# Seven-product steps of a decoder trunk: four weight sums by VectorE subtractions, against three VectorE additions and one accumulating DMA

## The chip, the core and the metric

The kernel runs on one core of a Trainium2 chip. The metric is the device time of one execution in microseconds (us), the median over runs. Before the change it is 2035.99 us (3 runs, 2035.79 to 2036.19).

Names of the engines in the profile: PE is TensorE (PEld its weight loads), DVE is VectorE, ACT is ScalarE, POOL is GpSimd, SP is the engine that issues most DMAs here.

## What is computed

A decoder trunk of two layers over a sequence of 256 tokens with a model width of 2048, all in float32:

```
for l in range(DEPTH):                                   # 2
    h = rms_norm(x, norm1_g[l])
    z = h @ w_in[l]                                      # 2048 x 5120
    ... attention heads and gated groups -> mix
    x = x + mix @ w_out[l]                               # 2048 x 2048
    h2 = rms_norm(x, norm2_g[l])
    x = x + jnp.square(jax.nn.relu(h2 @ w_up[l])) @ w_down[l]   # 2048 x 8192, 8192 x 2048
return rms_norm(x, final_g)
```

The change is inside the product with `w_down`.

## The kernel before

**Splitting.** Each float32 weight and activation is split into a high part (`hi`, rounded to the fast matmul type by an ACT copy, line 160) and a low part (`lo`, the value less its high part, a DVE subtraction, line 170). A product is three matmuls: hi x hi, hi x lo, lo x hi. The weights come in blocks of 128 x 1024 numbers (512 KB), one DMA per block from the SP queue (line 151) into a `raw` buffer, of which there are six. There are seven `hi` buffers and six `lo` buffers. A block's `raw` buffer is free again when its `lo` is made.

**Steps.** The program is a list of steps. An ordinary step has one block: 24 matmuls of 128 x 256. A *seven-product step* (function `fast`) has two loaded blocks, which hold a 2 x 2 grid of weight sub-blocks, and makes 7 instead of 8 sub-products of it by the Strassen-Winograd scheme: 7 products of 6 matmuls each. For that it needs four sums of weights. They are made in place in the two loaded blocks, and the two blocks are then split a second time as if they were new blocks. So a seven-product step has four entries in the list of blocks: before the change `Top`, `Bottom`, and two `Sums`, here called *upper* and *lower*. Each entry takes one `hi` and one `lo` buffer. The activations' sums (function `sums`) and the final combination of the seven products (function `combine`) are made by DVE too. The seventh product of a step is left over and done inside the next step.

**Where they stand.** In each layer the MLP runs over nine rounds `e` (0 to 8); round `e` has 16 ordinary steps for `w_up` and works on the hidden columns of round `e - 1` for `w_down`: in rounds 1 to 7 four seven-product steps and 8 ordinary steps, in round 8 two and 12. That is 30 seven-product steps in a layer, 60 in all. In rounds 2 to 7 they are put ahead of the `w_up` steps numbered 1, 2, 6 and 13, so the first two of them have a single ordinary step between them. In round 1 they stand at 7, 10, 14 and 15.

**What sets the order.** Each engine runs its instructions in the order in which the program issues them. Ahead of a step's matmuls the program calls `high_to`, which issues ACT copies for blocks up to six entries ahead, and then `low_to`, which issues DVE subtractions up to five entries ahead (fewer at the program's start). The entries of a `Sums` first issue the DVE sums, and ahead of these `high_to` makes sure that the low parts which still need the unsummed block are issued. Other work (updates of `x`, the `relu` square of the hidden columns at lines 733, 734, 629, 630, the sum of kept products at line 805) is put between the steps by small queues.

Of the kernel before, what the change touches and what calls it, by code (L numbers as in the profile page):

```python
# [85 lines left out]
def trunk(ctx: ExitStack, tc: tile.TileContext, layout, xT, consts, gains, w, b_sp, w_sp, out):  # L86
    nc = tc.nc
# [9 lines left out]
    vec, act, pe = nc.vector, nc.scalar, nc.tensor  # L97
# [9 lines left out]
    inner = ar[:, 0:2048].rearrange("p (k t) -> p k t", k=NH)  # L107
# [29 lines left out]
    class Sub:  # L137


        loads, frees = True, 1  # L140

        def __init__(self, *spec):
            self.i = len(layout)
            self.kc, self.n = spec[-2:]
            layout.append(spec)
# [7 lines left out]
        def high(self, parts, between=None):  # L153
            self.h = wp.tile([P, 1024], F32R, name="hi", tag="hi", bufs=HI_BUFS)
            self.hi = self.h.rearrange("p (k n) -> p k n", n=self.n)
            m = 1024 // parts
            for j in range(parts):
                if between and j:
                    between()
                act.activation(self.h[:, j * m:(j + 1) * m], self.raw[:, j * m:(j + 1) * m], AF.Copy)  # L160

        def low(self, parts, between=None):
            lo = wp.tile([P, 1024], F32R, name="lo", tag="lo", bufs=LO_BUFS)
            self.lo = lo.rearrange("p (k n) -> p k n", n=self.n)
            m = 1024 // parts
            for j in range(parts):
                r = slice(j * m, (j + 1) * m)
                if between and j:
                    between()
                vec.tensor_tensor(lo[:, r], self.raw[:, r], self.h[:, r].bitcast(F32), op=OP.subtract)  # L170

    class Top(Sub):


        def high(self, parts):
            h = wp.tile([P, 1024], F32R, name="hi", tag="hi", bufs=HI_BUFS)
            self.hi = h[:, 0:512].rearrange("p (k n) -> p k n", k=2)
            act.activation(self.hi, self.left(), AF.Copy)

        def low(self, parts):  # L180
            lo = wp.tile([P, 1024], F32R, name="lo", tag="lo", bufs=LO_BUFS)
            self.lo = lo[:, 0:512].rearrange("p (k n) -> p k n", k=2)
            vec.tensor_tensor(self.lo, self.left(), self.hi.bitcast(F32), op=OP.subtract)

        def left(self):
            return self.raw.rearrange("p (k n) -> p k n", k=2)[:, :, 0:256]

        def right(self):
            return self.raw.rearrange("p (k n) -> p k n", k=2)[:, :, 256:512]

        frees = 0

    class Bottom(Sub):


        left, right, frees = Top.left, Top.right, 0

    class Sums(Sub):


        loads = False

        def __init__(self, top, bottom, second):
            self.top, self.bottom, self.second = top, bottom, second
            self.n = 512

        def high(self, parts):
            t, b = self.top, self.bottom
            if self.second:
                vec.tensor_tensor(b.right(), b.right(), t.left(), op=OP.subtract)  # L210
                vec.tensor_tensor(b.left(), b.right(), b.left(), op=OP.subtract)
            else:
                vec.tensor_tensor(t.left(), t.right(), t.left(), op=OP.subtract)
                vec.tensor_tensor(t.right(), b.right(), t.right(), op=OP.subtract)  # L214
            self.raw = (b if self.second else t).raw
            Sub.high(self, 1)


# [1 line left out]
    cols = cp.tile([P, (2 * DEPTH + 1) * KC + 2 * DEPTH * NH], F32, name="cols")  # L220
# [14 lines left out]
    def later(delay, cost, fn):  # L235

        queue.append((now[0] + delay, cost, fn))
# [160 lines left out]
    def fast(name, l, row0, col0, tiles, slots, fresh, last, done):  # L398

        o = []
        for p in range(2):
            top, bottom = (cls(name, l, row0 + (4 * h + 2 * p) * P, col0, 2, 512) for h, cls in enumerate((Top, Bottom)))
            upper, lower = Sums(top, bottom, False), Sums(top, bottom, True)

            def mm(p=p, top=top, bottom=bottom, upper=upper, lower=lower):
# [5 lines left out]
                left, right = slice(0, 256), slice(256, 512)  # L414

                def product(n, a, lower_rows, tt, b, cols):
                    for k in range(2):
                        xh, xl = (a[:, 4 * lower_rows + 2 * p + k, i, tt * P:(tt + 1) * P] for i in range(2))
                        hi, lo = b.hi[:, k, cols], b.lo[:, k, cols]
                        pe.matmul(o[n], lhsT=xh, rhs=hi, start=(p == 0 and k == 0 and n in fresh), stop=False,  # L420
                                  skip_group_check=True)
                        pe.matmul(o[n], lhsT=xh, rhs=lo, start=False, stop=False, skip_group_check=True)  # L422
                        pe.matmul(o[n], lhsT=xl, rhs=hi, start=False, stop=(last and p == 1 and k == 1),  # L423
                                  skip_group_check=True)
# [6 lines left out]
            steps.append(((top, bottom, upper, lower), mm, (lambda: done(o)) if p and done else None))  # L431

    def natural(name, l, col0, ncols, after):

# [62 lines left out]
    def layer(l, n1, n2, n3, last):  # L497
# [245 lines left out]

        def sums():

            a11, a12, a21, a22 = (inner[:, 4 * k:4 * k + 4, t * P:(t + 1) * P] for t in range(2) for k in range(2))
            vec.tensor_tensor(a22, a21, a22, op=OP.add)
            vec.tensor_tensor(a21, a11, a21, op=OP.subtract)
            vec.tensor_tensor(a11, a22, a11, op=OP.subtract)
            vec.tensor_tensor(a12, a12, a11, op=OP.subtract)  # L750

            def parts(k):
                to_half(sum_parts[0], k, inner[:, k:k + 2, :])
                summed[0] = k == 6

            for k in range(0, 8, 2):
                later(0, 0.6, lambda k=k: parts(k))

        def combine(o, c, banks, final):
            p1, p2, p3, p5, p7, p6, p4 = o  # L760
# [5 lines left out]
            vec.tensor_tensor(u, u, p5, op=OP.add)  # L766
            vec.tensor_tensor(c12, u, p3, op=OP.add)
            vec.tensor_tensor(c21, c22, p4, op=OP.subtract)
            vec.tensor_tensor(c22, c22, p5, op=OP.add)
# [43 lines left out]
        for e in range(9):  # L813
# [3 lines left out]
            if e:  # L817
                w = sum(FAST[:1 + (e < 8)])
# [35 lines left out]
    n_load, n_high, n_low, n_raw = [0], [0], [0], [0]  # L854
# [50 lines left out]
    done = 0  # L905
# [24 lines left out]
    n = norms[-1]  # L930
# [3 lines left out]
    for c, w in [(0, 1), (1, 1)] + [(c, 2) for c in range(2, KC, 2)]:  # L934
        r = slice(c, c + w)
# [38 lines left out]
```

## Time and profile before

| | |
|---|---|
| median of the runs | 2035.99 us |
| time of the profiled execution | 2035.95 us |
| its span, first to last instruction | 2034.2 us |
| around the span | 1.75 us |
| mean granted TensorE clock | 0.997 |
| PE busy | 2022.1 us, 99% |
| DVE busy | 1583.7 us, 78% |
| ACT busy | 1051.9 us, 52% |
| POOL busy | 68.4 us, 3% |
| DMA, share of 16 engines, hardware queue of SP | 56.3% |
| HBM read | 390.65 MB |

Busy shares are averages over the span. Whether an engine's work or a wait matters is read from the stretch where it stands: the timeline of an engine gives start and length of each instruction, and in brackets the idle time before it and what ended that.

### The profile page before, as it was taken

To read this page: it belongs to the slowest core of one execution; us is meant where nothing else is said; L and a number is where in the kernel's file an instruction comes from. 1 tells how busy PE (TensorE), PEld (TensorE's weight loads), DVE (VectorE), ACT (ScalarE), POOL (GpSimd) and SP (SyncE) were. 2 spreads that over 40 slices of the span, in tenths; PEclk is the share of its full clock that TensorE was granted. 3 is DMA by queue.
4 is the path that set the end of the run, shared out by engine and by line. 5 is a ranking of instruction groups with operands and counts; after the bars stand their busy time and mean duration, and the time that the engine had idled before them with its cause. 6 is when DMAs were issued, how large, how long until landed. Compare 5 with 4: busy or idle time off the path is not lost.

```text
span 2034.2 us, 40532 instructions
## 1 busy us (share of the span) xinstructions
PE 2022.1 (99%) x16914; PEld 1985.8 (98%) x16914; DVE 1583.7 (78%) x1970; ACT 1051.9 (52%) x1325; POOL 68.4 (3%) x90
## 2 busy tenths in 40 slices
PE   9999999999999999999999999999999999999997
PEld 8998999999999999999989989999999999999997
DVE  7666766798888888888865667668988888888896
ACT  7565444455545455454645554545554544545444
POOL 0002300000000000000000032000000000000000
PEclk9999999999999999999999999999999999999998
DMA  8545555565564655646574455554665565555653
GB/s 318 190 166 166 187 188 199 174 208 197 192 229 164 225 188 194 229 161 213 187 237 157 169 184 186 187 199 166 205 205 200 207 206 187 199 197 208 207 181 110
DMA packets 112136, 395.39 MB, mean 194 GB/s; under 512 B 12368, under 2 KB 16464, under 8 KB 111952
## 3 DMA queue, kind: packets, MB, share of 16 engines
q1 hardware_dynamic: 110800, 389.86, 56.3%
q8 instruction: 132, 2.16, 0.4%
q10 hardware_dynamic: 1152, 2.94, 0.4%
q14 instruction: 52, 0.43, 0.1%
HBM read 390.65 MB, written 2.10 MB: 193 GB/s over the span
## 4 chain that ended last, share of the span: by engine, by line
PE 99%; DVE 0%; DMA 0%; ACT 0%; issue 0%; ACTq 0%; DVEq 0%
PE acc L391 25%; PE acc L395 25%; PE acc L393 25%; PE acc L449 3%; PE acc L451 3%; PE acc L450 3%; PE aux L420 3%; PE aux L422 3%; PE aux L423 3%; PE acc L423 2%; PE acc L420 2%; PE acc L422 2%; PE aux L675 0%; PE aux L619 0%; PE aux L577 0%; PE aux L606 0%
## 5 line engine op out<-in xcount | busy, mean ns | idle before, releaser
L160 ACT ACTIVATE hi<-raw 128x1024 fp32r<-128x1024 f32 (+1 forms) x801 | 807.3, 1047 | 468.8 <-DVE raw L214 190.3
L170 DVE TENSOR_TENSOR lo<-raw,hi 128x1024 fp32r<-128x1024 f32 (+1 forms) x801 | 944.9, 1216 | 48.2 <-ACT hi L160 31.3
L391 PE MATMUL acc<-hs,hi 128*128 128x256 f32 x2816 | 782.1, 278 | 0.0
L395 PE MATMUL acc<-hs,hi 128*128 128x256 f32 x2816 | 779.3, 277 | 0.0
L393 PE MATMUL acc<-hs,lo 128*128 128x256 f32 x2816 | 779.2, 277 | 0.0
L393 PEld LDWEIGHTS acc<-hs,lo 128*128 128x128 f32 x2816 | 528.9, 188 | 0.4 <-issue 0.2
L391 PEld LDWEIGHTS acc<-hs,hi 128*128 128x128 f32 x2816 | 528.9, 188 | 0.3 <-issue 0.2
L395 PEld LDWEIGHTS acc<-hs,hi 128*128 128x128 f32 x2816 | 528.7, 188 | 0.0
L391 PE MATMUL acc<-half,hi 128*128 128x256 f32 x1600 | 442.9, 277 | 0.0
L395 PE MATMUL acc<-half,hi 128*128 128x256 f32 x1600 | 442.4, 276 | 0.0
L393 PE MATMUL acc<-half,lo 128*128 128x256 f32 x1600 | 442.4, 276 | 0.0
L393 PEld LDWEIGHTS acc<-half,lo 128*128 128x128 f32 x1600 | 300.5, 188 | 0.0
L395 PEld LDWEIGHTS acc<-half,hi 128*128 128x128 f32 x1600 | 300.4, 188 | 0.0
L391 PEld LDWEIGHTS acc<-half,hi 128*128 128x128 f32 x1600 | 300.4, 188 | 0.0
L629 ACT ACTIVATE half<-ar 128x512 fp32r<-128x512 f32 x72 | 45.6, 634 | 187.3 <-DVE ar L734 172.8
L733 DVE TENSOR_TENSOR ar<-acc,nR 128x512 f32<-128x512 f32 x64 | 44.1, 689 | 86.9 <-PE acc L395 86.9
L489 DVE TENSOR_TENSOR x<-x,acc 128x512 f32<-128x512 f32 (+1 forms) x89 | 60.3, 677 | 65.9 <-PE acc L395 65.9
L449 PE MATMUL acc<-hi,hs 128*128 128x512 f32 x256 | 101.6, 397 | 0.1
L451 PE MATMUL acc<-hi,hs 128*128 128x512 f32 x256 | 100.6, 393 | 0.0
L450 PE MATMUL acc<-lo,hs 128*128 128x512 f32 x256 | 100.2, 391 | 0.0
L630 DVE TENSOR_TENSOR half<-ar,half 128x512 fp32r<-128x512 f32 x72 | 49.9, 693 | 50.4 <-ACT half L629 50.4
L277 ACT ACTIVATE hs<-x,cols 128x256 fp32r<-128x256 f32 x64 | 29.2, 501 | 90.8 <-DVE x L489 90.0
(150 smaller groups left out, 2252.2 us busy)
## 6 DMA issues: line engine op xcount, KB each, us to landing
raw<-in_w SPq DMA_DIRECT2D x731, 512.0 KB, 4.5
raw<-in_w SPq DMA_DIRECT2D x10, 256.0 KB, 4.8
x<-in_xT SPq DMA_DIRECT2D x7, 256.0 KB, 5.5
out<-x SPq DMA_DIRECT2D x7, 256.0 KB, 3.1
shared<-in_b_sp ACTq DMA_DIRECT2D x2, 512.0 KB, 7.8
shared<-in_w_sp ACTq DMA_DIRECT2D x2, 512.0 KB, 10.0
con<-in_consts ACTq DMA_DIRECT2D x1, 512.0 KB, 7.7
x<-in_xT ACTq DMA_DIRECT2D x2, 128.0 KB, 4.0
```

The lines of the kernel that those rows point to most:

```text
L160: act.activation(self.h[:, j * m:(j + 1) * m], self.raw[:, j * m:(j + 1) * m], AF.Copy)
L170: vec.tensor_tensor(lo[:, r], self.raw[:, r], self.h[:, r].bitcast(F32), op=OP.subtract)
L391: pe.matmul(o, lhsT=hi, rhs=xs[:, 0, :], start=(k0 + k == 0 and (two or cb == 0)), stop=False, skip_group_check=True)
L393: pe.matmul(o, lhsT=wt.lo[:, k, cb * P:(cb + 1) * P], rhs=xs[:, 0, :], start=False, stop=False, skip_group_check=True)
L395: pe.matmul(o, lhsT=hi, rhs=xs[:, 1, :], start=False, stop=last, skip_group_check=True)
L420: pe.matmul(o[n], lhsT=xh, rhs=hi, start=(p == 0 and k == 0 and n in fresh), stop=False, skip_group_check=True)
L422: pe.matmul(o[n], lhsT=xh, rhs=lo, start=False, stop=False, skip_group_check=True)
L423: pe.matmul(o[n], lhsT=xl, rhs=hi, start=False, stop=(last and p == 1 and k == 1), skip_group_check=True)
L449: pe.matmul(ps, lhsT=xh, rhs=hi, start=(k0 + k == 0), stop=False)
L450: pe.matmul(ps, lhsT=xh, rhs=lo, start=False, stop=False)
L451: pe.matmul(ps, lhsT=xl, rhs=hi, start=False, stop=(k0 + k == KC - 1))
L489: vec.tensor_tensor(xj, xj, ps[j][:, 0:S] if alone else pair(ps)[:, j, :], op=OP.add)
```

## The change

The two loaded blocks are cut differently: before, `Top` and `Bottom` each hold two row groups and all 512 columns, so that a sub-block is a strided half of a block; now `Left` and `Right` each hold four row groups and 256 columns, so that a sub-block is a contiguous half: `[:, 0:512]` (u) and `[:, 512:1024]` (v). The signs of the scheme are turned so that all four sums of weights are additions:

- v of right becomes v + u of right (DVE),
- u of right becomes u of right + u of left: a DMA from the POOL queue reads u of left once more from HBM (256 KB) and adds it onto u of right in place,
- u of left becomes u of left + the new v of right (DVE),
- v of left becomes v of left + the new u of left (DVE).

The two `Sums` are here called *first* (from the left block) and *second* (from the right block). All three DVE additions and the DMA are issued ahead of the ACT copy of *first*; the second `Sums` issues no sum of its own. `high_to` now issues the low parts up to and including the entry just ahead of a `Sums`, so the low part of *first* is issued ahead of the ACT copy of *second*. The order of the seven products changes with the scheme, and `sums` and `combine` change signs and operands with the same number of instructions.

```
+    class Right(Sub):
+        frees = 0
         def high(self, parts):
             h = wp.tile([P, 1024], F32R, name="hi", tag="hi", bufs=HI_BUFS)
-            self.hi = h[:, 0:512].rearrange("p (k n) -> p k n", k=2)
-            act.activation(self.hi, self.left(), AF.Copy)
+            self.hi = h.rearrange("p (k n) -> p k n", k=4)
+            act.activation(h[:, 512:1024], self.raw[:, 512:1024], AF.Copy)
...
     class Sums(Sub):
         def high(self, parts):
-            t, b = self.top, self.bottom
-            if self.second:
-                vec.tensor_tensor(b.right(), b.right(), t.left(), op=OP.subtract)
-                vec.tensor_tensor(b.left(), b.right(), b.left(), op=OP.subtract)
-            else:
-                vec.tensor_tensor(t.left(), t.right(), t.left(), op=OP.subtract)
-                vec.tensor_tensor(t.right(), b.right(), t.right(), op=OP.subtract)
-            self.raw = (b if self.second else t).raw
+            a, r = self.left.raw, self.right.raw
+            u, v = slice(0, 512), slice(512, 1024)
+            if not self.second:
+                vec.tensor_tensor(r[:, v], r[:, v], r[:, u], op=OP.add)
+                nc.gpsimd.dma_start(r[:, u], w[self.left.i][:, u], accum_op=OP.add)
+                vec.tensor_tensor(a[:, u], a[:, u], r[:, v], op=OP.add)
+                vec.tensor_tensor(a[:, v], a[:, v], a[:, u], op=OP.add)
+            self.raw = r if self.second else a
             Sub.high(self, 1)
...
-                        (half, 0, 0, top, left), (half, 1, 0, bottom, left), (extra, 1, 0, bottom, right),
-                        (extra, 1, 1, upper, left), (extra, 0, 1, upper, right), (extra, 0, 0, lower, right))):
+                        (half, 0, 0, le, 0), (half, 1, 0, le, 1), (extra, 1, 0, ri, 1),
+                        (extra, 0, 0, first, 0), (half, 1, 1, first, 1), (extra, 0, 1, second, 1))):
                     product(n, *args)
-                left_over.append(lambda: product(6, half, 1, 1, lower, left))
+                left_over.append(lambda: product(6, extra, 1, 1, second, 0))
...
             if not subs[n_high[0]].loads:
-                low_to(n_high[0] - 1)
+                low_to(n_high[0])
             subs[n_high[0]].high(parts)
```

**On VectorE**, at the second of the two close seven-product steps of round 4 in layer 0 (the stretch whose times the prediction shows). Before, from the low half of `Top` (L183; the block is raw_7137) over the sums of *upper* (L213, L214) and *lower* (L210, L211, block raw_7172) to the next ordinary block (lo_7453) and the sum of kept products (L805):

```order
L170 TENSOR_TENSOR lo_7356<-raw_7102,hi_7323 128x1024
L183 TENSOR_TENSOR lo_7399<-raw_7137,hi_7354 128x512
L213 TENSOR_TENSOR raw_7137<-raw_7137 128x2x256
L214 TENSOR_TENSOR raw_7137<-raw_7172,raw_7137 128x2x256
L170 TENSOR_TENSOR lo_7405<-raw_7172,hi_7397 128x1024
L210 TENSOR_TENSOR raw_7172<-raw_7172,raw_7137 128x2x256
L211 TENSOR_TENSOR raw_7172<-raw_7172 128x2x256
L170 TENSOR_TENSOR lo_7413<-raw_7137,hi_7403 128x1024
L170 TENSOR_TENSOR lo_7415<-raw_7172,hi_7409 128x1024
L170 TENSOR_TENSOR lo_7453<-raw_7203,hi_7411 128x1024
L805 TENSOR_TENSOR ar_78<-ar_78,acc0_7360 128x512
```

Now (lines 205, 207 and 208 are the three additions, 190 the low half of `Right`; raw_7137 is the left block, raw_7172 the right one):

```order
L170 TENSOR_TENSOR lo_7356<-raw_7102,hi_7323 128x1024
L170 TENSOR_TENSOR lo_7399<-raw_7137,hi_7354 128x1024
L190 TENSOR_TENSOR lo_7401<-raw_7172,hi_7397 128x512
L205 TENSOR_TENSOR raw_7172<-raw_7172 128x512
L207 TENSOR_TENSOR raw_7137<-raw_7137,raw_7172 128x512
L208 TENSOR_TENSOR raw_7137<-raw_7137 128x512
L170 TENSOR_TENSOR lo_7409<-raw_7137,hi_7407 128x1024
L170 TENSOR_TENSOR lo_7415<-raw_7172,hi_7411 128x1024
L170 TENSOR_TENSOR lo_7453<-raw_7203,hi_7413 128x1024
L799 TENSOR_TENSOR ar_78<-ar_78,acc0_7360 128x512
```

One of the four sums is gone, and the low parts of both loaded blocks now stand ahead of all sums, where before the low part of `Bottom` stood between the two pairs of sums.

**On ScalarE**, the copies of the same step. Before (L178 the half of `Top`, then `Bottom`, *upper*, *lower*, and three ordinary blocks):

```order
L178 ACTIVATE hi_7354<-raw_7137 128x512
L160 ACTIVATE hi_7397<-raw_7172 128x1024
L160 ACTIVATE hi_7403<-raw_7137 128x1024
L160 ACTIVATE hi_7409<-raw_7172 128x1024
L160 ACTIVATE hi_7411<-raw_7203 128x1024
L160 ACTIVATE hi_7451<-raw_7296 128x1024
```

Now (`Left`, the half of `Right` at line 185, *first*, *second*, and the same ordinary blocks):

```order
L160 ACTIVATE hi_7354<-raw_7137 128x1024
L185 ACTIVATE hi_7397<-raw_7172 128x512
L160 ACTIVATE hi_7407<-raw_7137 128x1024
L160 ACTIVATE hi_7411<-raw_7172 128x1024
L160 ACTIVATE hi_7413<-raw_7203 128x1024
L160 ACTIVATE hi_7451<-raw_7296 128x1024
```

The order is the same; the copy of *second* (hi_7411) now reads a half that the DMA wrote, and the copies of the ordinary blocks stand behind it.

**On POOL**, between the last work of layer 0's gated groups and the first of layer 1. Now:

```order
L337 TENSOR_SCALAR rt<-rt 128x8
L338 TENSOR_TENSOR lr<-lr,rt 128x8
L659 TENSOR_SCALAR shared<-shared,mv,lr 128x128 x8
L206 DMA raw<-in_w 128x512 x30
L503 TENSOR_TENSOR shared<-shared,con 128x1024
L328 TENSOR_SCALAR lr<-rt 128x8
```

The 30 accumulating DMAs of a layer stand in one run, with no other POOL work between them; before there was nothing at that place.

More of the change, by code (lines that the diff above doesn't have):

```diff
@@ L170, in low @@
                 vec.tensor_tensor(lo[:, r], self.raw[:, r], self.h[:, r].bitcast(F32), op=OP.subtract)
-    class Top(Sub):
+    class Left(Sub):
+        frees = 0
+    class Right(Sub):
+        frees = 0
         def high(self, parts):
             h = wp.tile([P, 1024], F32R, name="hi", tag="hi", bufs=HI_BUFS)
-            self.hi = h[:, 0:512].rearrange("p (k n) -> p k n", k=2)
-            act.activation(self.hi, self.left(), AF.Copy)
+            self.hi = h.rearrange("p (k n) -> p k n", k=4)
+            act.activation(h[:, 512:1024], self.raw[:, 512:1024], AF.Copy)
@@ L180, in low @@
         def low(self, parts):
             lo = wp.tile([P, 1024], F32R, name="lo", tag="lo", bufs=LO_BUFS)
[L182 to L196, printed above, removed]
+            self.lo = lo.rearrange("p (k n) -> p k n", k=4)
@@ L404, in fast, with mm @@
         for p in range(2):
-            top, bottom = (cls(name, l, row0 + (4 * h + 2 * p) * P, col0, 2, 512) for h, cls in enumerate((Top, Bottom)))
-            upper, lower = Sums(top, bottom, False), Sums(top, bottom, True)
-            def mm(p=p, top=top, bottom=bottom, upper=upper, lower=lower):
+            le, ri = (cls(name, l, row0 + 4 * p * P, col0 + 256 * h, 4, 256) for h, cls in enumerate((Left, Right)))
+            first, second = Sums(le, ri, False), Sums(le, ri, True)
+            def mm(p=p, le=le, ri=ri, first=first, second=second):
                 if p == 0:
@@ L413, in mm, with product @@
                 extra = sum_parts[0]
-                left, right = slice(0, 256), slice(256, 512)
-                def product(n, a, lower_rows, tt, b, cols):
+                def product(n, a, lower_rows, tt, b, below):
                     for k in range(2):
-                        xh, xl = (a[:, 4 * lower_rows + 2 * p + k, i, tt * P:(tt + 1) * P] for i in range(2))
-                        hi, lo = b.hi[:, k, cols], b.lo[:, k, cols]
+                        xh, xl = (a[:, 4 * p + 2 * lower_rows + k, i, tt * P:(tt + 1) * P] for i in range(2))
+                        hi, lo = b.hi[:, 2 * below + k, :], b.lo[:, 2 * below + k, :]
                         pe.matmul(o[n], lhsT=xh, rhs=hi, start=(p == 0 and k == 0 and n in fresh), stop=False,
@@ L426, in mm @@
                 for n, args in enumerate((
-                        (half, 0, 0, top, left), (half, 1, 0, bottom, left), (extra, 1, 0, bottom, right),
-                        (extra, 1, 1, upper, left), (extra, 0, 1, upper, right), (extra, 0, 0, lower, right))):
+                        (half, 0, 0, le, 0), (half, 1, 0, le, 1), (extra, 1, 0, ri, 1),
+                        (extra, 0, 0, first, 0), (half, 1, 1, first, 1), (extra, 0, 1, second, 1))):
                     product(n, *args)
-                left_over.append(lambda: product(6, half, 1, 1, lower, left))
-            steps.append(((top, bottom, upper, lower), mm, (lambda: done(o)) if p and done else None))
+                left_over.append(lambda: product(6, extra, 1, 1, second, 0))
+            steps.append(((le, ri, first, second), mm, (lambda: done(o)) if p and done else None))
     def natural(name, l, col0, ncols, after):
@@ L744, in sums @@
         def sums():
-            a11, a12, a21, a22 = (inner[:, 4 * k:4 * k + 4, t * P:(t + 1) * P] for t in range(2) for k in range(2))
-            vec.tensor_tensor(a22, a21, a22, op=OP.add)
+            halves = inner.rearrange("p (a k c) t -> p k a c t", a=2, k=2)
+            a11, a12, a21, a22 = (halves[:, k, :, :, t * P:(t + 1) * P] for t in range(2) for k in range(2))
+            vec.tensor_tensor(a22, a21, a22, op=OP.subtract)
             vec.tensor_tensor(a21, a11, a21, op=OP.subtract)
             vec.tensor_tensor(a11, a22, a11, op=OP.subtract)
-            vec.tensor_tensor(a12, a12, a11, op=OP.subtract)
+            vec.tensor_tensor(a12, a12, a11, op=OP.add)
             def parts(k):
@@ L759, in combine @@
         def combine(o, c, banks, final):
-            p1, p2, p3, p5, p7, p6, p4 = o
+            p1, p2, p3, p6, p4, p7, p5 = o
             b1, u, c11, c12, c21, c22 = (blocks[:, n, :] for n in range(6))
@@ L765, in combine @@
             vec.tensor_tensor(c22, u, p7, op=OP.add)
[L766 to L769, printed above, removed]
+            vec.tensor_tensor(u, u, p5, op=OP.subtract)
+            vec.tensor_tensor(c12, p3, u, op=OP.subtract)
+            vec.tensor_tensor(c21, c22, p4, op=OP.add)
+            vec.tensor_tensor(c22, p5, c22, op=OP.subtract)
             later(2, 1.5, lambda: turn_back(c, c11, c21, banks[0], final))
```

7 lines of the change are left out of this document (4 added, 3 removed).

## The prediction

> **What bounds the kernel now.** I read the page first (busy times, chain), then sums over stretches, then the timelines of DVE, ACT and PE at the seven-product steps.
>
> ```profile
> PE   2022.1 (99%) x16914; PEld 1985.8 (98%) x16914; DVE 1583.7 (78%) x1970; ACT 1051.9 (52%) x1325; POOL 68.4 (3%) x90
> PE 99%; DVE 0%; DMA 0%; ACT 0%; issue 0%; ACTq 0%; DVEq 0%
> 5.70:2021.00 2015.30, 2015.27 (x16880) 1979.51 (x16881) 1577.16 (x1953) 1047.98 (x1318) 68.17 (x86) 1.00 0.57 195
> 549.00:633.50 84.50, 84.50 (x746) 84.50 (x745) 70.91 (x82) 42.79 (x48) 0.00 (x0) 1.00 0.57 199
> ```
>
> The last two rows are the stretch with its length, then busy time of PE, PEld, DVE, ACT and POOL, the clock, and the DMA share. PE is busy 2015.27 of 2015.30 us between its first weights and the end of its products, and the chain is PE alone. The change leaves the number of matmuls and their shapes as they are, so nothing can be gained there but 0.03 us; any wait that it puts before a matmul is lost whole. DVE's relief is therefore worth nothing by itself. One round (last row, 84.5 us, four seven-product steps) has 13.6 us free on DVE and 41.7 us on ACT. So the question is how early the last split of a step is ready, before and after.
>
> The tightest recurring place is the second of the two close steps of a round. DVE's timeline of round 4, then PE's:
>
> ```profile
> 624.06 0.68 DVE L183 TENSOR_TENSOR lo<-raw,hi 128x512 fp32r<-128x512 f32 x1
> 625.60 0.69 DVE L489 TENSOR_TENSOR x<-x,acc 128x512 f32<-128x512 f32 x1 [0.85 <-PE acc L395]
> 626.20 0.68 DVE L213 TENSOR_TENSOR raw<-raw 128x512 f32<-128x512 f32 x1
> ...
> 630.12 1.22 DVE L170 TENSOR_TENSOR lo<-raw,hi 128x1024 fp32r<-128x1024 f32 x1
> 631.25 0.68 DVE L489 TENSOR_TENSOR x<-x,acc 128x512 f32<-128x512 f32 x1
> 631.85 2.35 DVE L170 TENSOR_TENSOR lo<-raw,hi 128x1024 fp32r<-128x1024 f32 x2
> 634.12 0.68 DVE L183 TENSOR_TENSOR lo<-raw,hi 128x512 fp32r<-128x512 f32 x1
> 634.84 0.69 DVE L213 TENSOR_TENSOR raw<-raw 128x512 f32<-128x512 f32 x1
> 635.56 0.69 DVE L214 TENSOR_TENSOR raw<-raw 128x512 f32<-128x512 f32 x1
> ...
> 638.15 0.69 DVE L211 TENSOR_TENSOR raw<-raw 128x512 f32<-128x512 f32 x1
> 638.76 3.65 DVE L170 TENSOR_TENSOR lo<-raw,hi 128x1024 fp32r<-128x1024 f32 x3
> 645.38 0.69 DVE L805 TENSOR_TENSOR ar<-ar,acc 128x512 f32<-128x512 f32 x1 [2.96 <-PE acc L423]
> 641.10 0.28 PE L420 MATMUL acc<-hi,half 128*128 128x256 f32 x1
> 644.61 0.28 PE L422 MATMUL acc<-lo,shared 128*128 128x256 f32 x1
> 645.30 0.28 PE L393 MATMUL acc<-hs,lo 128*128 128x256 f32 x1
> ```
>
> The step that DVE prepares from 634.12 on starts on PE at 641.10. At 644.61 PE first reads the low part of *lower*, at 645.30 that of the next ordinary block. The last three splits run from 638.76 to 642.41, so *lower* is ready at 641.2, 3.4 us early. DVE then idles 2.96 us: that is the cover for whatever gets slower.
>
> **The DMA's time, called L** (POOL released, to data landed). No accumulating DMA and no POOL DMA is in this trace. The nearest rows:
>
> ```profile
> L344 POOL TENSOR_TENSOR lr<-lr,rt 128x8 f32<-128x8 f32 x12 | 6.6, 551 | 1.0
> out<-x SPq DMA_DIRECT2D x2, 128.0 KB, 1.7
> raw<-in_w SPq DMA_DIRECT2D x1, 512.0 KB, 4.4
> 631.36 10.27 SPq L151 DMA_DIRECT2D raw<-in_w  x5
> raw<-in_w SPq DMA_DIRECT2D x1, 512.0 KB, 3.3
> raw<-in_w SPq DMA_DIRECT2D x32, 512.0 KB, 4.6
> raw<-in_w SPq DMA_DIRECT2D x8, 512.0 KB, 5.7
> ```
>
> The first is a small POOL instruction (0.55 us, my floor for POOL's part). The others are DMAs, median us to landing: a small store at the end; the one load issued between 623 and 628; SP's next five issues, from 631.36 on, of which the first took 3.3, alone in flight; the 32 loads of a round; the 8 issued back to back between 657 and 667. The new DMA brings 256 KB from HBM and must also read 256 KB of the block onto which it adds, so I take a 512 KB load as its like. At the first close step it is issued near 627.6, when one load is still landing and the next comes 3.8 us later, hence a little over the lone 3.3: 3.65. With POOL's 0.55, L = 4.2 us. Ends: 0.55 + 1.7 = 2.3 and 0.55 + 5.7 = 6.3.
>
> The Trainium skill, page "DMA: Bandwidth & Descriptors", section "Anatomy of one DMA — SWDGE (gpsimd) path", fits a POOL-issued copy by 2.0 us plus bytes over 436 GB/s; for 256 KB that is an estimate of 2.6 us, by which the sum below would be zero. It is fitted to copies, not to adds, and no run shows it here.
>
> **The change, part by part.**
>
> *Removed: one DVE sum per step*, 60 in all at 0.69 us, 41 us of DVE. Off the path: worth 0.
>
> *Added: DVE waits for ACT.* The low part of *first* now stands right behind the last addition, while its ACT copy can only start there (one such copy and its release:)
>
> ```profile
> 627.72 1.07 ACT L160 ACTIVATE hi<-raw 128x1024 fp32r<-128x1024 f32 x1 [6.46 <-DVE raw L214]
> ```
>
> From the end of an addition to the end of the copy is 0.11 + 1.07 us, in which DVE idles; before, the copy of *upper* ran under the low part of `Bottom`. That eats the 0.69 us and some 0.5 more.
>
> *Added: ACT's copy of second waits for the DMA*, and behind it on ACT stand the copies of the ordinary blocks; behind the low part of *second* on DVE stand theirs. I replay the DVE row by row, with a spacing of 1.14 us per full split, 0.61 to 0.72 per half instruction:
>
> First close step: `Left` 624.06, the update of x at 625.60 as before, half of `Right` 626.20, first addition 626.92 to 627.61: POOL starts. Copy of *second* from 627.7 + L, ends 1.07 later; its low part starts at 628.85 + L (0.08 for the release), where it started at 631.85 before: a shift of L - 3.0. At L = 4.2 that is 1.2 us against a lead above 3: PE does not wait here, but DVE enters the second step 1.2 us late.
>
> Second close step, with S = 628.85 + L the start of that low part: next block S + 1.14, `Left` S + 2.28, half of `Right` S + 3.41, first addition S + 4.13 to S + 4.82; low part of *second* from S + 4.82 + 0.1 + L + 1.07 = S + L + 6.0 (DVE's own path, by way of *first*, gives S + 8.6, earlier for L above 2.6); the next block's low part ends 1.14 + 1.22 later, at S + L + 8.36 = 637.2 + 2L. PE wants it at 645.30. **Wait = 2L - 8.1**: zero up to L = 4.05; 0.3 us at 4.2. This holds for rounds 3 to 7 (five steps a layer).
>
> Round 1 has less lead. Its first step:
>
> ```profile
> 388.68 0.68 DVE L183 TENSOR_TENSOR lo<-raw,hi 128x512 fp32r<-128x512 f32 x1
> 392.00 0.69 DVE L213 TENSOR_TENSOR raw<-raw 128x512 f32<-128x512 f32 x1
> 395.91 1.22 DVE L170 TENSOR_TENSOR lo<-raw,hi 128x1024 fp32r<-128x1024 f32 x1
> 399.71 0.28 PE L422 MATMUL aux<-lo,shared 128*128 128x256 f32 x1
> ```
>
> `Left` takes 0.5 us more than the half of `Top`, so the half of `Right` stands at 392.5, the first addition ends at 393.95, the low part of *second* starts at 395.15 + L and the next block's ends at 397.5 + L; PE wants that 0.69 us after 399.71. Wait = L - 2.9: 1.3 us. Two more are taken like it, the last step of round 1 (one DMA behind, about L - 3.2: 1.0) and the second close step of round 2 (0.6 us less lead than the steady one: 2L - 7.5: 0.9). All others have the update of the hidden columns between *first* and *second*, or 1.5 us and more to spare at L = 4.2: zero.
>
> *Moved and unpriced:* 60 x 256 KB more HBM reads, 15.7 MB on 390.65, at a DMA share of 0.57: covered by the load's own lead; `raw` of the right block comes free up to 2 us later, and the load behind it with it, covered while six buffers hold; if that cover goes, ACT waits for loads next. POOL has no other work between its DMAs. `sums`, `combine`: same counts, zero.
>
> **Sum** per layer: 1.3 + 1.0 + 0.9 + 5 x 0.3 = 4.7; two layers 9.4. On the profiled execution's own time, 2035.95 us (span 2034.2 and 1.75 around it, 0.04 below the median of the runs): 2045 us, 0.5% slower. The measurement tells apart about 0.2%, 4.1 us.
>
> **Rivals.**
> 1. *Not slower*: the add costs no more than a lone load. At L = 3.9 the sum is 2 x (1.0 + 0.7 + 0.3) = 4.0 us, within 0.2%; below 2.9 it is zero. For it: the lone load's 3.3 us, only one or two loads in flight then. Against: POOL's part, and the second read. Time 2036. The skill's fit above would put it here.
> 2. *Much later data*: L of 5.6 or more. For it: the back-to-back loads' 5.7 us; and two more additions (0.69 us each) start on DVE just as POOL begins, so that if POOL's making of the transfer stood back for them, L would be 4.2 + 1.4 = 5.6. Sum at 5.6: 2 x (2.7 + 2.4 + 3.7 + 5 x 3.1) = 49 us, 2085; at 6.3, 2 x (3.4 + 3.1 + 5.1 + 5 x 4.5) = 68 us, 2104, and more where steps with ample lead begin to wait. Against: those 8 loads queue behind each other. The Trainium skill, page "SBUF — State Buffer", section "Who interferes with whom", has a two-input DVE instruction hold up POOL's reads of SBUF, but infers that making a DMA's descriptors is not held up; this trace has no POOL DMA to show it.
> 3. *Faster*: only if matmuls themselves ran quicker from contiguous halves; PE's 0.03 us of idle leaves no other way. I see nothing for it.
>
> **Chances.** The forecast, L from 3.9 to 5.6, 2040 to 2088: 0.47. Rival 1: 0.37. Rival 2: 0.13. Rival 3: 0.03. Faster by over 0.2%: 0.03; within: 0.37; slower: 0.60. The range runs from 2034 (no wait at all) to 2090, leaving out most of rival 2 and of rival 3.
>
> **What would show it.** Right: POOL DMAs that land about 4 us after their issue; ACT copies at line 160 that wait for them; PE idle before the low-part matmuls (lines 387 and 415 of the changed code) of round 1, and a few tenths in the second close step of each later round. PE busy unchanged near 2022, DVE about 41 us less. Rival 1: the same ACT waits, PE's idle unchanged. Rival 2: PE idle of 2 us and more in every round, DVE waiting for ACT. I am wrong if L is as I say and PE still never waits (then DVE's slack was larger than I replayed), or if loads, not copies, become late.

## The result and the profile after

The changed kernel takes 2058.03 us (median of 4 runs, 2055.51 to 2064.41) against 2036.09 (4 runs beside it, 2035.79 to 2036.23): a ratio of 1.0113, 95% interval 1.0100 to 1.0125. The forecast was 2045, so the sign and the range hold and the size does not: 22 us were lost and 9.4 were forecast. The ratios leave out single runs more than 1.5% above a kernel's fastest; below, where a kernel's times fall into groups, I give the times instead.

The profiled execution is the longest of the four: 2064.41 us, span 2062.6, which is 28.4 us over the span before. From its page, and the stretch between PE's first weights and the end of its products:

```profile
PE 2039.5 (99%) x16914; PEld 1995.8 (97%) x16914; DVE 1548.0 (75%) x1910; ACT 1050.3 (51%) x1325; POOL 120.1 (6%) x150
L206 POOL DMA_DIRECT2D raw<-in_w x60 | 52.1, 868 | 1471.9 <-DVE raw L205 1044.0
raw<-in_w POOLq DMA_DIRECT2D x60, 256.0 KB, 3.8
```

```profile
5.80:2049.00 2043.20, 2032.04 (x16871) 1988.90 (x16872) 1541.04 (x1892) 1046.09 (x1317) 119.90 (x146) 1.00 0.61 200
```

PE has the same 16,914 matmuls. In its stretch it now idles 11.2 us (2043.20 less 2032.04), where it idled 0.03. But "PE busy" has also grown, from 2022.1 to 2039.5 us, with no matmul added. So part of the loss is not idle time in these columns: behind a wait the first matmul is longer (0.38 or 0.39 us where the others have 0.28, in the rows below), and elsewhere matmuls stand further apart. The forecast had PE busy unchanged near 2022 us. DVE has 60 instructions less, as forecast, and 36 us less busy time, where 41 were forecast; it is worth nothing.

The waits (engine, tile and line, what is waited for; us in total, times, longest):

```profile
ACT hi L160 <- DMA raw<-in_w: 140.7, 111, 3.3
DVE lo L170 <- ACT hi L160: 133.8, 111, 3.7
PEld acc L387 <- DVE lo L170: 9.2, 20, 2.4
PEld acc L415 <- DVE lo L170: 6.4, 11, 1.1
PEld aux L415 <- DVE lo L170: 2.1, 2, 1.1
```

This is the forecast chain: the DMA holds ACT's copy, ACT holds DVE's subtraction, DVE holds PE's low-part matmuls at lines 387 and 415. The second close step of round 4 in layer 0, which the prediction replayed, in the timelines of DVE, POOL, ACT and PE:

```profile
640.55 3.50 DVE L170 TENSOR_TENSOR lo<-raw,hi 128x1024 fp32r<-128x1024 f32 x3 [0.81 <-ACT hi L160]
...
644.68 0.69 DVE L205 TENSOR_TENSOR raw<-raw 128x512 f32<-128x512 f32 x1
...
651.29 2.36 DVE L170 TENSOR_TENSOR lo<-raw,hi 128x1024 fp32r<-128x1024 f32 x2 [2.03 <-ACT hi L160]
645.90 0.86 POOL L206 DMA_DIRECT2D raw<-in_w  x1 [9.26 <-DVE raw L205]
650.19 5.81 ACT L160 ACTIVATE hi<-raw 128x1024 fp32r<-128x1024 f32 x6 [2.19 <-DMA raw<-in_w]
653.70 0.38 PE L387 MATMUL acc<-hs,lo 128*128 128x256 f32 x1
```

The first addition ends at 645.37 and POOL starts its DMA 0.53 us later. The data is there just before 650.19, when ACT starts the copy of *second*: L is 4.7 here. The low part of *second* starts at 651.29. By the replay it should start 1.18 + L behind the addition, at about 651.25.

**Where the 28.4 us are.** I set the start of every matmul of this execution against the same-numbered one before and sorted the additional distances by step; a distance that grew by more than 30 ns counts as a wait, the rest as a changed spacing. The middle column feeds the prediction's formulas with each DMA's own L, read from the trace.

| us, both layers | forecast, L = 4.2 | formulas, each DMA's own L | measured |
|---|---|---|---|
| first step of round 1, L - 2.9 | 2.6 | 3.1 | 3.4 |
| last step of round 1, L - 3.2 | 2.0 | 2.2 | 3.6 |
| second close step of round 2, 2L - 7.5 | 1.8 | 1.6 | 2.1 |
| second close step of rounds 3 to 7, 2L - 8.1 | 3.0 | 8.0 | 8.0 |
| other steps | 0 | 0 | 5.5 |
| matmuls further apart, no wait | 0 | 0 | 6.3 |
| sum | 9.4 | 14.9 | 28.9 |

(The span grew by 28.4 us: some 0.5 us come back outside the two MLPs.) L over the 60 DMAs has a median of 4.3 and a mean of 4.5; it runs from 4.05 to 5.8. Over the 20 DMAs of the close pairs in rounds 3 to 7 its mean is 4.45, and no pair is on time: by the formula their waits run from 0.2 to 1.9 us.

That the two 8.0 agree is partly chance. Eight of the ten pairs measure about 0.1 us more than the formula. The two of rounds 4 and 5 in layer 0 measure some 0.55 us less; they stand in the stretch with slower matmuls described below, where PE asks for the data later.

Of the 5.5 us in other steps, 4.0 are one place, the last seven-product step of layer 0. PE's row, DVE's rows, and three stretches (length, PE, PEld, DVE, ACT, POOL, clock, DMA share):

```profile
1000.47 0.39 PE L387 MATMUL acc<-half,lo 128*128 128x256 f32 x1 [2.21 <-DVE lo L170]
995.99 1.23 DVE L170 TENSOR_TENSOR lo<-raw,hi 128x1024 fp32r<-128x1024 f32 x1 [1.81 <-PE aux L415]
997.13 0.68 DVE L482 TENSOR_TENSOR x<-x,acc 128x512 f32<-128x512 f32 x1
998.39 0.88 DVE L275 SCALAR_TENSOR_TENSOR hs<-x,cols,hs 128x256 fp32r<-128x256 f32 x2 [0.58 <-ACT hs L271]
999.19 4.62 DVE L170 TENSOR_TENSOR lo<-raw,hi 128x1024 fp32r<-128x1024 f32 x4
998.00:1000.40 2.40, 0.25 (x3) 0.05 (x1) 2.01 (x4) 2.40 (x5) 0.00 (x0) 1.00 0.68 218
1000.40:1004.60 4.20, 4.13 (x22) 4.14 (x23) 4.20 (x5) 4.20 (x6) 0.00 (x0) 0.59 0.62 202
1004.60:1008.80 4.20, 4.20 (x39) 4.20 (x39) 4.03 (x10) 0.63 (x1) 0.00 (x0) 1.00 0.97 353
```

DVE came late out of this step, and the next block's low part then stood behind an update of `x` and two writes of the next layer's `hs`. PE idled 2.21 us, and right behind that the granted clock fell: the 4.2 us from 1000.40 on hold 22 matmuls at a mean clock of 0.59, the next 4.2 us hold 39. That costs about 2 us more, as much as the wait.

Of the 6.3 us without a wait, 6.1 are in one stretch:

```profile
570.00:740.00 170.00, 170.00 (x1445) 169.88 (x1445) 131.12 (x149) 80.39 (x91) 6.92 (x8) 1.00 0.62 202
745.00:990.00 245.00, 244.67 (x2147) 244.06 (x2146) 201.16 (x232) 120.64 (x138) 9.52 (x11) 1.00 0.65 211
```

Both have PE busy all the time and a granted clock of 1.00. In the first a matmul takes 117.6 ns (170.00 / 1445), in the second 114 (245.00 / 2147, two waits in it). Before, the whole MLP ran at 113.3 to 113.9. The slow spacing begins at a wait of PE (564.8) and ends at one (741.0). The much smaller wait at 653.70, which cost 0.2 us, stands inside it and did not end it. I had not foreseen it, and the experiments had to tell what it is.

### The profile page after: what moved, and what is told of

Same layout as the page of the kernel before. It is cut to its first block, busy times and chain, and to the rows that moved or that the text cites. A ratio compares the mean times of both kernels' runs of the same rounds, so it can differ in the third digit from the quotient of the medians.

```text
span 2062.6 us, 40714 instructions
## 1 busy us (share of the span) xinstructions
PE 2039.5 (99%) x16914; PEld 1995.8 (97%) x16914; DVE 1548.0 (75%) x1910; ACT 1050.3 (51%) x1325; POOL 120.1 (6%) x150
## 5 line engine op out<-in xcount | busy, mean ns | idle before, releaser
L206 POOL DMA_DIRECT2D raw<-in_w x60 | 52.1, 868 | 1471.9 <-DVE raw L205 1044.0
L415 PE MATMUL aux<-lo,shared 128*128 128x256 f32 x312 | 86.9, 278 | 1.7 <-DVE lo L170 1.7
```

The costliest lines, as they stand in the source:

```text
L206: nc.gpsimd.dma_start(r[:, u], w[self.left.i][:, u], accum_op=OP.add)
```

## The experiments

Each edit is against the changed kernel unless it says otherwise. The kernel before ran beside each: 2036.07 us beside experiments 1 to 4 (22 runs, 2035.63 to 2036.94), 2036.07 beside 5 to 8 (19 runs, 2035.58 to 2036.70), and 2036.19 (one run) beside the two further executions of 7 and 8.

**1. The sum by DVE, no DMA.**

```
-                nc.gpsimd.dma_start(r[:, u], w[self.left.i][:, u], accum_op=OP.add)
+                vec.tensor_tensor(r[:, u], r[:, u], a[:, u], op=OP.add)
```

> The accumulating DMA is replaced by a fourth DVE addition (u of right plus u of left) at its place in the order; everything else is the changed kernel. Theory A (late data: ACT's copy of second waits for the DMA, 4.3 us after the first addition's end, and PE waits for the low parts behind it): no DMA to wait for; DVE has 0.7 us more per step; the replay leaves at most some tenths of a wait in round 1: 2036 to 2038 us, PE idle back below 1 us in the products. Theory B (issue order: the low part of first stands right behind the additions, so DVE waits 1.2 us for ACT in every step): that wait stays and DVE has 0.7 us more, so as slow as the change or slower, 2058 us or more. Theory C (the 15.7 MB of extra reads and POOL's work make the block loads late): 2036 us, as A.

Measured: 2074.79 us median (2059.06 to 2075.58), ratio 1.0172, interval 1.0136 to 1.0208: three of its four runs are longer than any of the changed kernel, without its DMA. Two groups of PE's waits in this kernel, then two stretches of it and the same two of the kernel before:

```profile
PEld acc L387 <- DVE lo L170: 1.2, 3, 0.5
PEld aux L415 <- DVE lo L170: 0.6, 2, 0.3
```

```profile
500.00:900.00 400.00, 400.00 (x3402) 400.00 (x3401) 323.64 (x371) 192.20 (x218) 0.00 (x0) 1.00 0.56 194
1500.00:1900.00 400.00, 400.00 (x3402) 400.00 (x3401) 326.59 (x369) 198.17 (x223) 0.00 (x0) 1.00 0.56 194
```

```profile
500.00:900.00 400.00, 400.00 (x3522) 400.00 (x3521) 334.62 (x384) 203.52 (x230) 0.00 (x0) 1.00 0.57 199
1500.00:1900.00 400.00, 400.00 (x3522) 400.00 (x3522) 336.06 (x386) 201.30 (x227) 0.00 (x0) 1.00 0.59 201
```

Matched against the kernel before, PE's waits are only 3.5 us in all (2.8 in the MLP), with the slower first matmuls behind them, so theory A was right that the late data goes with the DMA. But 35.8 us are lost with PE busy, at clock 1.00: 3402 matmuls in 400 us (117.6 ns) against 3522 (113.6). B's number came out, but not by B's mechanism: DVE's order does not make PE wait here. A itself was incomplete; call the slow spacing theory D.

**2. The same bytes, added onto an unused buffer.** The u half of right stays unsummed.

```
-                nc.gpsimd.dma_start(r[:, u], w[self.left.i][:, u], accum_op=OP.add)
+                for j in (0, 256):
+                    nc.gpsimd.dma_start(aside, w[self.left.i][:, j:j + 256], accum_op=OP.add)
```

> The DMA stays in number of bytes and place but adds onto an unused buffer (two transfers of 128 KB each, since there is room for no more), and nothing waits for it; u of right stays unsummed, so that sum is left out of the computation. Theory A: 2036 to 2037 us. Theory B: 2058 us, since DVE's order and its wait for ACT are as in the change. Theory C: 2050 to 2060 us, since traffic and POOL work stay.

Measured: 2036.95 us (2036.02 to 2038.48), ratio 1.0005, interval 0.9996 to 1.0014. With the traffic, the new order of DVE and ACT, but nobody waiting for the DMA, nothing is lost:

```profile
aside<-in_w POOLq DMA_DIRECT2D x120, 128.0 KB, 4.9
500.00:900.00 400.00, 400.00 (x3522) 400.00 (x3521) 322.74 (x365) 201.82 (x229) 6.92 (x8) 1.00 0.59 201
1500.00:1900.00 400.00, 400.00 (x3523) 400.00 (x3522) 323.57 (x365) 199.16 (x226) 6.92 (x8) 1.00 0.60 204
```

The matmuls stand 113.6 ns apart. Theories B and C are refuted by this run: neither the order alone nor the 15.7 MB cost anything that shows (0.9 us between the medians, and the interval holds 1). What costs is that something waits for the late sum.

**3. A plain copy in place of the add** (`accum_op` left out, so u of right becomes u of left), and **4. half the columns by the DMA**, the other half by a DVE addition of 0.4 us:

```
-                nc.gpsimd.dma_start(r[:, u], w[self.left.i][:, u], accum_op=OP.add)
+                nc.gpsimd.dma_start(r[:, 0:256], w[self.left.i][:, 0:256], accum_op=OP.add)
+                vec.tensor_tensor(r[:, 256:512], r[:, 256:512], a[:, 256:512], op=OP.add)
```

> The same POOL DMA of the same 256 KB to the same place, but as a plain copy; the addition of u of right is left out. Same waits on it. Theory A with the add as the dear part (data read back and added): landing falls from 3.8 to about 3.0 us after issue, 3.5 after the addition's end, below where the close steps begin to wait (7.9 us for two), so 2037 to 2041 us. Theory A with the add for free: landing stays at 3.8 us and the time at 2054 to 2062 us. The Trainium skill, page DMA: Bandwidth & Descriptors, section Anatomy of one DMA, would have an estimate of 2.6 us for the copy.

> The DMA adds only 256 of the 512 columns (128 KB), a DVE addition of 0.42 us does the other half; same waits. If the landing time is mostly bytes: 3.8 us falls to about 2.6, and the time to 2036 to 2039 us. If it is mostly a fixed cost (POOL 0.86 us, start and end of a transfer): it falls to 3.4 us at most, and the time to 2040 to 2050 us.

Measured: the copy 2049.35 us (ten runs from 2039.54 to 2074.88), the half 2057.16 (seven runs: three from 2042.06 to 2044.19, four from 2057.16 to 2060.79). The DMAs of each (KB, us to landing) and the largest group of waits of PE:

```profile
raw<-in_w POOLq DMA_DIRECT2D x60, 256.0 KB, 2.9
PEld acc L387 <- DVE lo L170: 2.6, 6, 1.1
```

```profile
raw<-in_w POOLq DMA_DIRECT2D x60, 128.0 KB, 3.1
PEld acc L388 <- DVE lo L170: 3.5, 7, 1.3
```

From the end of the first addition to the landed data the copy takes 3.5 us (median), the half 3.6, with DVE held 0.4 us longer by its extra addition, and the full add 4.3. The waits of PE in the profiled executions follow that: 4.1, 6.5 and 22.6 us. The rest of these two profiles is the slow spacing, 16.1 and 18.8 us, nearly all of layer 0. By the time to landing, the copy's first expectation came out (2.9 us, 3.0 expected) and the half's second (3.1 us, at most 3.4 expected): half the bytes took off 0.7 of 3.8 us. Four of the copy's ten runs (2039.54 to 2041.92) lie within 1 us of 2037 to 2041, and the half's three short runs in 2040 to 2050; the others are longer. So theory A holds for the waits, and the times do not follow the waits alone.

**5. The DMA issued early**, right behind the load of its block, where it waits for no DVE addition; the signs are set for that (the two sums of the left block become a subtraction and an addition).

```
+        def load(self, parts):
+            Sub.load(self, parts)
+            nc.gpsimd.dma_start(self.raw[:, 0:512], w[self.left.i][:, 0:512], accum_op=OP.add)
```

> The accumulating DMA is issued right behind the load of its block, which is in flight 9 to 13 us ahead of the first addition at the close pairs and 3 to 5 us at the other steps; the four sums then begin with an addition that needs the landed sum, and no addition stands ahead of the DMA. Theory A (PE loses the waits for late sums, and nothing else): the 4.3 us of the DMA lie inside the slack of the load, no wait of PE over 0.5 us at the places where the changed kernel waits, 2036 to 2040 us. Theory D (a wait of PE leaves its matmuls 117.7 ns apart in place of 113.5 until the next wait, on top of A): 2036 to 2040 us as long as no wait is left at all; with even one wait of a few tenths it can be 2042 to 2058. Theory B (DVE's order with the two-operand sums is what costs): 2050 or more.

Measured: 2077.14 us (2075.45 to 2079.84), ratio 1.0203, interval 1.0188 to 1.0218. The times of theories A and D were missed. B's "2050 or more" came out, but the traces show PE waiting for late data again. The second step of round 1 in layer 0, POOL, DVE and PE:

```profile
402.22 0.87 POOL L184 DMA_DIRECT2D raw<-in_w  x1 [21.77 <-DVE lo L170]
403.91 0.68 DVE L194 TENSOR_TENSOR lo<-raw,hi 128x512 fp32r<-128x512 f32 x1
410.42 0.69 DVE L209 TENSOR_TENSOR raw<-raw 128x512 f32<-128x512 f32 x1 [5.83 <-DMA raw<-in_w]
416.34 0.58 PE L419 MATMUL aux<-lo,half 128*128 128x256 f32 x1 [2.29 <-DVE lo L170]
```

The DMA now runs among the loads that SP issues in a row, five of them in flight, and lands 8.1 us after its issue; over all 60 it takes 3.5 to 8.1 us, median 4.9. At the close pairs of rounds 2 to 7 DVE asks for the sum 7.8 to 10.4 us after POOL's start, the DMA takes 3.6 to 5.4, and PE lost nothing in either layer: theory A holds where its condition does. But at the second step of round 1 in both layers DVE's first addition waited for the DMA, PE idled over 2 us and the clock fell: 6.8 and 6.5 us in all at that step. In layer 0 DVE was ready for the sum at 404.59, 2.4 us after POOL's start; I had counted on a DMA of 4.3 us inside a slack of 3 to 5. Nine other steps lost 0.5 to 4.0 us each, and slow spacing took 17 us more.

**6. The close pair pulled apart**: the step ahead of the ordinary step numbered 2 is put ahead of 3.

```
-            at = {1: (7, 10, 14, 15), 8: (0, 2)}.get(e, (6, 13, 1, 2))
+            at = {1: (7, 10, 14, 15), 8: (0, 2)}.get(e, (6, 13, 1, 3))
```

> The changed kernel with one partial step of each round put one place later, so that two steps with a load no longer stand next to each other. Theory A: the waits of the second close step (0.8 us in the mean in rounds 3 to 7, 1.05 in round 2, ten and two of them) go, about 10 us of the 22; those of round 1 and the last steps stay, or move: 2042 to 2050 us. Theory D: the same waits, but which of the rest sets off the slow cadence decides: 2042 to 2075, and the time follows the matmuls at 117.7 ns, not the sum of the waits.

Measured: 2105.47 us (2104.19 to 2108.17), ratio 1.0342: far outside all expectations. Two groups of waits, a wait of PE in round 3, and the stretch behind it:

```profile
PE acc L385 <- DVE ar L799: 31.8, 12, 3.3
PEld acc L415 <- DVE lo L170: 2.4, 3, 1.1
578.74 0.55 PE L385 MATMUL acc<-hs,hi 128*128 128x256 f32 x1 [2.99 <-DVE ar L799]
578.70:582.00 3.30, 3.26 (x15) 3.29 (x16) 2.57 (x4) 2.16 (x4) 0.00 (x0) 0.50 0.48 87
```

The waits for low parts at line 415 fell from 6.4 us in 11 to 2.4 in 3, and those at line 387 from 9.2 in 20 to 4.7 in 8, as the pairing in "2L" demands. But a new wait came with the move: in the twelve rounds 2 to 7 PE stood some 2.7 us in the mean for an accumulator that the sum of kept products (line 799) had not read out yet, and in nine of them the clock halved after it. This run says nothing against the 2L, and little for it.

**7. Waits alone, in the kernel before**: three needless additions on DVE ahead of the sums of the first step of round 1 in layer 0, and of one step late in layer 1. No DMA, no new order; `scratch` stands for a buffer that nothing reads there.

```
+            if not self.second:
+                for _ in range(PAUSE.get(at[0], 0)):        # PAUSE = {0: 3, 48: 3}
+                    vec.tensor_tensor(scratch, con[:, 0:512], con[:, 0:512], op=OP.add)
+                at[0] += 1
```

> The kernel before, with three needless additions on DVE (0.69 us each, 2.1 us) ahead of the sums of two steps only: the first step of round 1 in layer 0, and the third step of round 5 in layer 1, whose operands are ready 1.1 us ahead of need; the rest is untouched. PE waits some 1 us at each. Theory A (a wait costs its own length and the refill, 0.3 us): 2038 to 2039 us. Theory D: behind the first wait the matmuls stand 117.7 ns apart up to the end of layer 0 (about 540 us of matmuls, 3.7% of it 19 us), behind the second to the end of layer 1 (about 7 us): up to 2063, and 2045 or 2056 if one of the two sets it off; with matmuls at 113.5 ns throughout, D falls.

> The same kernel as the one with three needless additions at two steps, looked at once more (its ten times lay at 2038.4 to 2039.0 and 2056.6 to 2057.5). Theory D: at 2057 the matmuls from the first wait to the end of layer 0 stand 117.7 ns apart, none of the rest does, and the waits are 1.3 us each as before. Theory T: matmuls at 113.5 ns and some 18 us of other waits. At 2038 the look tells nothing between the two.

Measured: six of ten runs at 2038.38 to 2038.97, four at 2056.56 to 2057.48; a further execution, the second with a profile, gave 2057.28. So one program has two times, 18 us apart, as D said for the first of the two waits. The second wait, in layer 1, cost 1.3 us too in both profiles, but none of the eleven executions shows the 7 us that D would add for it. PE's first wait and a stretch of layer 0 and one behind it; the shorter execution, then the longer:

```profile
399.38 0.39 PE L428 MATMUL aux<-lo,shared 128*128 128x256 f32 x1 [0.73 <-DVE lo L171]
402.00:945.00 543.00, 543.00 (x4777) 542.96 (x4778) 464.08 (x535) 278.53 (x314) 0.00 (x0) 1.00 0.58 201
960.00:1500.00 540.00, 540.00 (x4329) 522.30 (x4329) 392.34 (x519) 281.31 (x379) 34.41 (x43) 1.00 0.56 187
```

```profile
399.82 0.39 PE L428 MATMUL aux<-lo,shared 128*128 128x256 f32 x1 [0.73 <-DVE lo L171]
402.00:945.00 543.00, 542.96 (x4614) 542.76 (x4614) 447.12 (x512) 271.20 (x305) 0.00 (x0) 1.00 0.57 197
960.00:1500.00 540.00, 540.00 (x4330) 522.30 (x4328) 393.50 (x519) 281.35 (x382) 33.94 (x43) 1.00 0.55 189
```

The wait is the same, 0.73 us, and costs 1.31 in both. Behind it the matmuls stand 113.7 ns apart in one (543 / 4777) and 117.7 in the other (543 / 4614), at the same clock of 1.00. That ends near 953, right behind a group of four transposes and not at a wait of PE; from there on they agree. Matched matmul by matmul, the longer execution has 2.8 us of waits and 18.7 of spacing; the shorter 2.6 and 0.05. That is D, and it refutes T, further waits.

By the start of each matmul the two traces say more than D does. Right behind the first wait the spacing is slow in both: the next 16 distances have 117.8 ns in the shorter, up to 401.49, and 117.9 in the longer, up to 401.93. Then PE waits again, 0.2 us, for the first low part of the ordinary block. From 403.2 on the shorter execution stands at 113.3 and the longer stays slow. So the same wait brought the slow spacing both times, and what differs is whether it went again within 4 us. Experiment 1 shows the like: behind its first wait, at 399.30, the spacing is slow and gone by 403; the long stretch begins at 414.83, where one distance is only 0.06 us longer than before the change. One weight load in three, that of line 397, is longer (both from 600 to 700, the shorter first):

```profile
L397 PEld LDWEIGHTS acc<-hs,hi 128*128 128x128 f32 x152 | 28.5, 188 | 0.0
```

```profile
L397 PEld LDWEIGHTS acc<-hs,hi 128*128 128x128 f32 x149 | 28.6, 192 | 0.0
```

**8. A long wait and a tiny one**, in the same manner: eight additions (PAUSE = {0: 8, 30: 2}).

> The kernel before, with eight needless additions on DVE (5.5 us) ahead of the sums of the first step of round 1 in layer 0, and two (1.4 us) ahead of those in layer 1. PE waits about 4 us at the first and 0.1 to 0.3 us at the second. Theory A: 2040 to 2041 us. Theory H (a wait of 2 us and more takes the granted clock to 0.5 for 3.4 us, as at the last step of layer 0 in the changed kernel): 2 us on top, 2042 to 2043, and the clock row shows it. Theory D: behind either wait matmuls 117.7 ns apart, 19 us for layer 0 and up to 18 for layer 1: 2060 to 2078.

> The same kernel as the one with eight and two needless additions, looked at once more, for a profile of one of its longer executions (its ten times lay at 2041.7 to 2043.2, 2060.8 to 2062.3 and 2079.0 to 2079.7). Theory D: at 2061 the matmuls of one layer, behind its wait, stand 117.7 ns apart at granted clock 1.00, at 2079 those of both; the waits themselves are as before, 5.4 and 0.7 us. A rival, T (the longer times come from transfers or from another engine): matmuls at 113.5 ns and further waits of PE, about 19 us a layer. At 2042 the look tells nothing between the two.

Measured: four of ten runs at 2041.65 to 2043.19, three at 2060.83 to 2062.25, three at 2078.96 to 2079.72: steps of about 19 and 18 us, as D has them for one layer each. That is inferred: the further execution gave 2042.72, so no long one has a profile here. Theory H is shown (PE's wait, then stretches of one of the shorter executions):

```profile
400.62 0.38 PE L428 MATMUL aux<-lo,half 128*128 128x256 f32 x1 [3.13 <-DVE lo L171]
401.50:404.90 3.40, 3.06 (x15) 2.77 (x15) 3.33 (x4) 2.77 (x3) 0.00 (x0) 0.50 0.19 52
404.90:408.00 3.10, 3.10 (x28) 3.10 (x28) 3.10 (x4) 2.66 (x4) 0.00 (x0) 1.00 0.87 278
```

Some 3 us idle, then 3.4 us at clock 0.50 with half the matmuls: 5.4 us lost at this step. The tiny wait in layer 1 cost 0.7 us.

## Why the prediction was right or wrong

**The bound and the sign: right.** PE had nothing to give, DVE's 36 us less were worth nothing, and waits before low-part matmuls at lines 387 and 415 were lost whole. The moved and unpriced rows (traffic, order) are zero by experiment 2.

**Which steps failed.** The mechanism was right; terms of the sum were too small. The profiled execution has 22.6 us of waits where the sum has 9.4. Of the 13.2 us between them 5.0 are the steady close steps, 5.5 the steps put at zero, 1.6 the last step of round 1, and 1.1 the first step of round 1 and the close step of round 2. What the sum had no term for at all is what a wait brings with it: a lower clock, about 2 of the 5.5 us, and the slow spacing, 6.3 us on top in this execution.

**L: too small by a quarter of a us, where that counts twenty times.** I took 0.55 for POOL and 3.65 to landing. The trace has 0.53 and a median of 3.8, so 4.3; in the close pairs of rounds 3 to 7 the mean of L is 4.45. There the term "0.3 us, five steps a layer" was to be 3.0 us; it measured 8.0. Its formula, 2L - 8.1, takes away nearly all of 2L, so what is left is small and an error in L enters twice in each of ten steps: 20 x 0.25 is the missing 5.0. With each DMA's own L (the sum of the two DMAs of the pair) the formula gives 8.0, and its longest case, DMAs of 5.7 and 4.3 us, 1.9 where the trace has 2.0. The 3.65 was read from a lone load and had no row of an adding DMA behind it.

**The last step of round 1: one DMA where two count.** L - 3.2 was "taken like" the first step and not replayed; 2.0 us were forecast and 3.6 measured, most of it in layer 1 (2.2). This step too is the second of a close pair, 14 and 15. DVE came into it late from the DMA of the step ahead, by way of ACT's copy; in layer 1:

```profile
1452.56 3.50 DVE L170 TENSOR_TENSOR lo<-raw,hi 128x1024 fp32r<-128x1024 f32 x3 [1.65 <-ACT hi L160]
```

The two DMAs of the pair took 9.5 us together in layer 0 and 10.0 in layer 1, and PE lost 1.4 and 2.2 us. The last DMA alone took 4.3 in both, which cannot tell the two layers apart.

**"All others zero": wrong.** I gave them the update of the hidden columns between *first* and *second*, or 1.5 us to spare. The last step of layer 0, whose following block stands behind work for the next layer on DVE, lost 4.0 us, half of it as a lower clock. The last steps of round 7 and two more, both in layer 1, lost 1.5 together.

**The price of a wait: wrong in kind.** I charged a wait at its own length. Experiments 7 and 8 show two surcharges. One is the clock at 0.5 for 3.4 us, which followed most gaps of 2.3 us and more between matmuls' starts. The other is the slow spacing, 3.7% on what stands behind the wait, which goes again within 4 us or stays: it lasted 176 us in the changed kernel and some 550 in experiment 7. In the profiled execution it took 6.3 us; without those it stands at 2058.1, near the other three (2055.5 to 2058.7). That these three had no slow spacing is inferred, since they have no profile.

**The rivals.** Rival 1 did not come: L of 2.9 or less would have been needed for no wait. The Trainium skill, page "DMA: Bandwidth & Descriptors", section "Anatomy of one DMA — SWDGE (gpsimd) path", has a fit for DMAs issued by POOL that gives an estimate of 2.6 us for 256 KB. Experiment 3 has 2.9 for the copy, near it; the add takes 3.8, and the section does not speak of adds. Rival 2 did not come either: POOL's part was 0.53 + 0.86 us beside both DVE additions, and the copy landed at 2.9 beside the same two, so the 1.4 us of holding up that this rival needs do not stand in it. Rival 3 did not come.

**Open:** what in the chip makes the slow spacing, and why the waits of the kernel before, outside the MLP, left no long stretch of it in 45 runs (none above 2036.94 us). Also open is what ends it: a wait at 741.0 in the changed kernel, four transposes near 953 in experiment 7. That it starts at waits is seen at the long stretches of the changed kernel and of experiments 1, 3, 4 and 7, down to hitches of 0.06 us; that it stays by chance, in the two times of one program. Its cause is not shown.

## What to carry to other kernels

Where one engine is the bound, price work moved to a DMA by the slack of each consumer. Where two such DMAs stand in a chain, their times add, and a small slack behind two long times makes the price sensitive: here a quarter of a us in the DMA's time was 5 us. So use the mean time of that kind of DMA among its neighbours, not that of a lone load, and replay the steps that seem to have slack. If the bound engine is TensorE, even a wait of a few tenths of a us is not cheap, since it can change the spacing of the matmuls for hundreds of us behind it. When times of one program fall into groups, compare matmuls per us in a stretch without waits before looking for a further stall.

## What was not expected of the hardware

- Two spacings of the same matmuls at clock 1.00: 113.6 and 117.7 ns, with every third weight load of the ordinary steps at 192 ns in place of 188. The slow one starts behind a wait of PE (0.7 us in experiment 7) or a hitch of 0.06 us (experiment 1), and goes again within 4 us or lasts, up to some 550 us. Behind the same wait it lasted in 5 of 11 executions of experiment 7, by their times; two of them have a profile, one of each kind.
- A gap of about 2.3 us between matmuls' starts was enough for the clock to halve (2.3 in experiment 6, with PE idle 2.0 us of it; 2.5 in the changed kernel, 2.2 idle), but two gaps of 3.5 us in experiment 6 passed without. The Trainium skill, page "TensorE: Matmul & The Clock Gate", section "Why this matters for your kernels", advises to keep PE's idle gaps below about 3 us; in these runs an idle gap of 2.0 us was already followed by the lower clock.
- An accumulating DMA of 256 KB takes 3.8 us to landing (median) where a copy takes 2.9. Its POOL instruction takes 0.86 us, also at 128 KB, against 0.54 for the copy.
